# Two score slots side by side in three PSUM banks, and a second bank for filling projections

## The chip, the cores and the metric

The program runs on one core of a Trainium2 chip. Its time is the device time of one execution in microseconds (us); less is better. Each profile is of one execution, and times in it count from the start of its span. Engines are called as the profile calls them: PE (TensorE matmuls), PEld (its weight loads), DVE (VectorE), ACT (ScalarE), POOL (GpSimd), SP (the queue that issues most DMAs). PSUM, where PE puts its results, has eight banks of 512 fp32 columns on each of 128 partitions.

## The reference

Two layers of a hybrid attention trunk on 512 latent and 256 context tokens, width 1024. One input projection feeds a neighbourhood attention (branch A) and a grouped-query attention (branch B); each is gated, projected, merged by sigmoid gates, and put through one output projection. The last layer keeps no context queries. What the change touches is branch B:

```python
def _attend(q, k, v):
    s = jnp.einsum('bqkgd,btkd->bkgqt', q, k).astype(jnp.float32) * (HEAD_DIM ** -0.5)
    p = jax.nn.softmax(s, axis=-1).astype(v.dtype)
    return jnp.einsum('bkgqt,btkd->bqkgd', p, v)
...
    k_all = jnp.concatenate([ckb, kb], axis=1)
    v_all = jnp.concatenate([cvb, vb], axis=1)
    b_att = _gqa_latent(qb, k_all, v_all)
...
    out_x = _merge(a_att, b_att, a_z, b_z, g_a, g_b, w_o_a, w_o_b, w_out)
    x_new = x + gate_x * out_x
```

So each of 8 query heads has 512 latent queries over 768 keys in both layers, and in layer 0 also 256 context queries over the 256 context keys.

## The kernel before

Every fp32 product is made of three matmuls of rounded high and low parts (L435 to L437, `mm3`), accumulated in one PSUM bank. A scheduler orders each engine's instructions when the program is built, by a time model of its own; at run time each engine goes through its list strictly in that order, and an instruction that waits holds up all behind it.

The stage that changes is the grouped-query attention, once per layer (L1144 to L1206). `pipeline` (L1017) goes over the heads: the scores of head h, then the values of head h-1, then a share of `fill`, a list of projections that have nothing to do with attention at that time (gate projections, then the output projection of branch A). The fill keeps PE busy while the softmax runs elsewhere.

A **score set** is 128 queries by 768 keys, made by `gq_scores` (L1152): four matmuls on PE (L890 and L891, two of 512 columns and two of 256) into a PSUM tile `pss`; DVE reads it for the row maxima (L1161); ACT reads it for the exponential (L1162), then casts the result to a high half (`h`, L841); POOL or DVE makes the low half (L842: DVE for the first and third set of a head, POOL for the second and fourth); a DMA transposes it into `ht` (L846). A head has four such sets. In layer 0 a fifth, smaller one follows (`ctx_scores`, L896): 128 by 512, its maxima on DVE at L903, two exponentials at L909. So there are 40 sets in layer 0 and 32 in layer 1.

The values of a head (`gq_values`, L1167) are four PE transposes of the sums (`divide`, L853) and twelve matmuls (L1178, L1179) into the two banks `t`; then ACT copies one half (`ho`, L828), DVE adds (L829), POOL or DVE multiplies into `zb` (L833). In layer 0 the context values (L925) use the bank `v`. After the last head, `hilo` (L667) splits `zb` (`gbh`, `gbl`), and the output projection of branch B starts.

The eight banks in this stage: one `f` and two `t` for the whole program (L101, L102), and what `open_ps` (L1145) gives: two score tiles `s` of 1024 columns, that is of two banks each, of which a set uses 768 columns, and one bank `v`. A filling projection takes its bank from `psw()` (L116). With only `f` to take, the next one starts when ACT's tanh (L625) or DVE's product (L627, L707) has emptied it; in layer 0 one single projection gets `v` instead (L1147).

## Time and profile before

| what | value |
|---|---|
| time of three runs | 1108.36 us median, 1107.52 to 1108.36 |
| profiled execution | 1111.07 us, span 1109.3 us, mean granted PE clock 0.991 |
| busy in the span | PE 1075.5 us, DVE 767.4, ACT 617.1, POOL 473.1 |
| HBM | 115.58 MB read, 17.32 MB written |
| first to last score set, layer 0 | 375.8 to 526.7 us |
| first to last score set, layer 1 | 923.7 to 1023.6 us |

The span is the time from the first to the last instruction in the profile; the profiled execution's own time is 1.8 us more. A busy PE is one with a matmul in flight: a matmul of 512 columns takes 0.39 us from start to end, but the next one starts 0.23 us after it. So what PE could do at best is counted by starts, and a wait of PE shows as a gap between starts. Views used: the busy times by stretch, the waits of one engine, the groups of instructions by line and shape, and the instructions in order of time.

### The profile page before, as it was taken

What the parts mean: (1) busy time and instruction counts of PE and PEld (TensorE: products, weight loads), DVE (VectorE), ACT (ScalarE), POOL (GpSimd) and SP (SyncE); (2) the same over time, 40 slices, a digit from 0 to 9 for tenths busy, and PEclk for the clock granted to TensorE, in tenths of its full rate; (3) what the DMA queues carried; (4) which work ended last, traced back from release to release, by engine and by line L of the source; (5) the groups of instructions that cost most, each with busy time, mean ns of one, the idle gap of its engine ahead of it and who ended that gap; (6) DMA issues with size and microseconds to landing.
All of it is one profiled execution on the core that took longest, in us unless ns stands there. A gap on an engine that the chain in (4) does not pass through costs nothing. (4 is left out here: it accounts for less than half of the span.)

```text
span 1109.3 us, 16937 instructions
## 1 busy us (share of the span) xinstructions
PE 1075.5 (97%) x5672; PEld 879.1 (79%) x5672; DVE 767.4 (69%) x1600; ACT 617.1 (56%) x1236; POOL 473.1 (43%) x397
## 2 busy tenths in 40 slices
PE   8999999999999989989999999999999999999998
PEld 5688888788888868767788878888877888777677
DVE  4667889975377487766777785366997665677473
ACT  6454279776433566765330275444899446786430
POOL 1054235555257154463621354232355472564531
PEclk9999999999999999998999999999999999999999
DMA  9455324554543379789633542453565536879642
GB/s 370 146 171 153 90 68 111 128 138 120 169 131 127 100 184 215 166 228 228 213 101 124 157 147 78 140 163 101 134 149 130 156 107 171 199 229 239 188 152 77
DMA packets 236000, 171.79 MB, mean 155 GB/s; under 512 B 160140, under 2 KB 201864, under 8 KB 234248
## 3 DMA queue, kind: packets, MB, share of 16 engines
q1 hardware_dynamic: 228576, 156.31, 51.6%
q0 software_dynamic: 2368, 7.87, 2.1%
q10 hardware_dynamic: 4968, 6.53, 1.8%
q8 instruction: 45, 0.74, 0.3%
q14 instruction: 43, 0.35, 0.1%
HBM read 115.58 MB, written 17.32 MB: 120 GB/s over the span
## 5 line engine op out<-in xcount | busy, mean ns | idle before, releaser
L842 POOL TENSOR_TENSOR h<-p,h 128x256 f16<-128x256 f32 (+2 forms) x104 | 113.6, 1101 | 160.0 <-ACT h L841 117.7
L422 POOL TENSOR_TENSOR wlo<-raw,whi 128x512 fp32r<-128x512 f32 x70 | 98.0, 1406 | 131.6 <-ACT whi L420 98.7
L435 PE MATMUL psf<-hx,whi 128*128 128x512 f32 (+1 forms) x360 | 138.2, 384 | 2.2 <-DVE zt L627 1.2
L436 PE MATMUL psf<-hx,whi 128*128 128x512 f32 (+1 forms) x360 | 136.1, 378 | 0.0
L437 PE MATMUL psf<-hx,wlo 128*128 128x512 f32 (+1 forms) x360 | 136.1, 378 | 0.0
L435 PE MATMUL psx<-whi,hx 128*128 128x512 f32 (+1 forms) x328 | 121.0, 372 | 0.0
L437 PE MATMUL psx<-whi,hx 128*128 128x512 f32 (+1 forms) x328 | 120.0, 367 | 0.0
L420 ACT CAST whi<-raw 128x512 fp32r<-128x512 f32 x136 | 83.2, 620 | 65.5 <-DMA raw<-in_w_in_dram 46.9
L436 PE MATMUL psx<-wlo,hx 128*128 128x512 f32 (+1 forms) x328 | 119.6, 366 | 0.0
L408 POOL TENSOR_TENSOR wlo<-raw,whi 128x512 fp32r<-128x512 f32 x40 | 59.8, 1499 | 117.7 <-ACT whi L405 74.6
L405 ACT CAST whi<-raw 128x512 fp32r<-128x512 f32 x88 | 54.3, 623 | 96.7 <-PE psx L437 34.2
L508 POOL TENSOR_TENSOR ss<-ss,ehalf 128x8 f32<-128x8 f32 (+2 forms) x40 | 63.6, 1593 | 77.2 <-DVE ss L505 72.2
L841 ACT CAST h<-p 128x256 f16<-128x256 f32 (+2 forms) x136 | 81.7, 616 | 5.3 <-DMA ht<-h 1.3
L422 DVE TENSOR_TENSOR wlo<-raw,whi 128x512 fp32r<-128x512 f32 x66 | 65.3, 992 | 25.9 <-ACT whi L420 24.3
L1161 DVE CUSTOM_DVE_ANT_0 p<-pss,vb 128x768 f32<-128x768 f32 x64 | 60.2, 953 | 31.0 <-PE pss L891 28.9
L1162 ACT ACTIVATE p<-pss,mx 128x768 f32<-128x768 f32 x64 | 57.6, 901 | 41.1 <-DVE mx L1161 40.4
L435 PEld LDWEIGHTS psf<-hx,whi 128*128 128x128 f32 x360 | 68.3, 190 | 14.9 <-ACT zt L625 1.9
L437 PEld LDWEIGHTS psf<-hx,wlo 128*128 128x128 f32 x360 | 68.2, 190 | 12.0
L436 PEld LDWEIGHTS psf<-hx,whi 128*128 128x128 f32 x360 | 68.3, 190 | 10.9
L437 PEld LDWEIGHTS psx<-whi,hx 128*128 128x128 f32 x328 | 61.9, 189 | 10.2
L436 PEld LDWEIGHTS psx<-wlo,hx 128*128 128x128 f32 x328 | 62.0, 189 | 9.5
L435 PEld LDWEIGHTS psx<-whi,hx 128*128 128x128 f32 x328 | 61.8, 189 | 9.1 <-issue 0.2
(338 smaller groups left out, 2984.7 us busy)
## 6 DMA issues: line engine op xcount, KB each, us to landing
raw<-in_w_in_dram SPq DMA_DIRECT2D x168, 256.0 KB, 3.0
rawb<-in_w_ada_dram SPq DMA_DIRECT2D x48, 256.0 KB, 2.8
raw<-in_w_out_dram SPq DMA_DIRECT2D x32, 256.0 KB, 2.9
tg<-gs SPq DMA_DIRECT2D x4, 1536.0 KB, 9.9
rawx<-in_w_ada_dram SPq DMA_DIRECT2D x4, 1024.0 KB, 10.3
rawy<-in_w_ada_dram SPq DMA_DIRECT2D x4, 1024.0 KB, 10.3
gs<-zt ACTq DMA_DIRECT2D x16, 256.0 KB, 2.6
raw<-in_w_o_a_dram SPq DMA_DIRECT2D x16, 256.0 KB, 3.1
```

What stands on the lines that cost most here:

```text
L405: S.copy(hi[:, :n], raw[:, :n])
L408: e.tensor_tensor(lo[:, :n], raw[:, :n], F(hi[:, :n]), ALU.subtract)
L420: S.copy(hi, raw)
L422: lo_eng(i).tensor_tensor(lo, raw, F(hi), ALU.subtract)
L435: T.matmul(ps, lhs[0], rhs[0], start=first, stop=False)
L436: T.matmul(ps, lhs[0], rhs[1], start=False, stop=False)
L437: T.matmul(ps, lhs[1], rhs[0], start=False, stop=last)
L508: G.tensor_tensor(ss, ss, ehalf[:, :n], ALU.pow)
L841: S.copy(h[:, 0], p[:, :n])
L842: eng.tensor_tensor(h[:, 1], p[:, :n], h[:, 0], ALU.subtract)
L1161: V.tensor_tensor_reduce(p, pss, lift, -1.0, 3e38, ALU.add, ALU.min, mx[:, 0:1])
L1162: S.activation(p, pss, AF.Exp, bias=mx[:, 0:1], accum_out=r[:, i:i + 1])
```

## The change

The PSUM of the stage is laid out anew. The two score tiles (two banks each, 768 of 1024 columns used) become one tile of 1536 columns, three banks, in which slot 0 is columns 0 to 767 and slot 1 is columns 768 to 1535. Banks end at columns 512 and 1024, so slot 0 has the first bank and half of the middle one, slot 1 the other half of the middle bank and the last. Matmuls are cut at the banks' ends: slot 0 as 512 and 256 columns, slot 1 as 256 and 512. The context set of layer 0 uses the first 512 columns of whichever slot's turn it is. The bank that is left becomes `x`, a second one besides `f` for filling projections, which now take turns; the single use of `v` for one of them goes. The line in `pipeline` keeps what it did, since its test by the number of banks would no longer tell the two attentions apart. No matmul, no DVE, ACT or POOL operation and no DMA of the computation is added or taken away.

```diff
             def ctx_scores(q, kh, kl, ct, late=True):
-                pss = ps_score()
+                pss = ps_slot()[0][:, 0:512] if late else ps_score()
...
-                    att["bg"] = bg if h > 3 or pm["n"] == 1 else []
+                    att["bg"] = bg if h > 3 or last is not None else []
...
-            open_ps(s=(2, 1024), v=(1, 512))
-            if first:
-                pm["v_for"] = (2,)
+            open_ps(x=1, s=(1, 1536), v=(1, 512))
+            slots = psw(1536, "s")
+            turn_of = [0]
+
+            def ps_slot():
+
+                i = turn_of[0] % 2
+                turn_of[0] += 1
+                return slots[:, 768 * i:768 * i + 768], (512, 256)[i]
...
-                    pss = ps_score(768)
+                    pss, m = ps_slot()
                     scores(pss, q[:, 128 * i:128 * i + 128], kh, kl,
-                           [(0, 512, cut(0, 512)), (512, 256, cut(512, 768))])
+                           [(0, m, cut(0, m)), (m, 768 - m, cut(m, 768))])
```

What the scheduler makes of it shows at three places. The lines below the insertion have moved by six (the maxima from L1161 to L1167, the exponential from L1162 to L1168, the values from L1178 and L1179 to L1184 and L1185).

The first place is PE in layer 1, in the middle of the stage; in brackets stand the engines whose semaphores a row waits for. Before, in the second head:

```order
L890 MATMUL pss_2042_9989<-gk_1884_9240,qs_2039_9984 128x512 [waits PE_49,Activation_49]
L891 MATMUL pss_2042_9989<-gk_1884_9240,qs_2039_9984 128x512
L890 MATMUL pss_2042_9989<-gk_1884_9240,qs_2039_9984 128x256
L891 MATMUL pss_2042_9989<-gk_1884_9240,qs_2039_9984 128x256
L890 MATMUL pss_2046_10002<-gk_1884_9240,qs_2039_9984 128x512 [waits PE_49,Activation_49]
L891 MATMUL pss_2046_10002<-gk_1884_9240,qs_2039_9984 128x512
L890 MATMUL pss_2046_10002<-gk_1884_9240,qs_2039_9984 128x256
L891 MATMUL pss_2046_10002<-gk_1884_9240,qs_2039_9984 128x256
L853 MATMUL pst_2058_10041<-ident_90,r4_2006_9851 128x128 [waits DVE_49]
L853 MATMUL pst_2058_10041<-ident_90,r4_2006_9851 128x128 x3
L435 MATMUL psf_2075_10117<-hx_1334_6680,whi_2024_9906 128x512 [waits Activation_49]
L436 MATMUL psf_2075_10117<-hx_1336_6682,whi_2024_9906 128x512
```

Of the changed kernel, the same engine and layer, from the fifth head's third set to the sixth head's first:

```order
L890 MATMUL pss_1967_9813<-gk_1846_9205,qs_2095_10408 128x512 [waits Activation_49]
L891 MATMUL pss_1967_9813<-gk_1846_9205,qs_2095_10408 128x512
L890 MATMUL pss_1967_9813<-gk_1846_9205,qs_2095_10408 128x256
L891 MATMUL pss_1967_9813<-gk_1846_9205,qs_2095_10408 128x256
L890 MATMUL pss_1967_9813<-gk_1846_9205,qs_2095_10408 128x256 [waits Activation_49]
L891 MATMUL pss_1967_9813<-gk_1846_9205,qs_2095_10408 128x256
L890 MATMUL pss_1967_9813<-gk_1846_9205,qs_2095_10408 128x512
L891 MATMUL pss_1967_9813<-gk_1846_9205,qs_2095_10408 128x512
L890 MATMUL pss_1967_9813<-gk_1846_9205,qs_2124_10525 128x512 [waits Activation_49]
L891 MATMUL pss_1967_9813<-gk_1846_9205,qs_2124_10525 128x512
L890 MATMUL pss_1967_9813<-gk_1846_9205,qs_2124_10525 128x256
L891 MATMUL pss_1967_9813<-gk_1846_9205,qs_2124_10525 128x256
```

Before, the two sets wait for two exponentials that both lie further back (each for the last set in its own tile), and 23 matmuls of a filling projection follow. After, three sets follow each other with nothing between them, and each waits for one exponential. Followed through the semaphore's counts, this is that of the set directly before it, in the other slot; of the 72 sets 70 wait so, and before each waits for the set two back. The last filling projection of this stage now stands ahead of the fourth head's first set; before, some stood behind the last head's scores.

The second place is DVE in layer 1, where the maxima (`p,mx<-pss`) stand among the low halves (`h<-p,h`). Before, in the sixth head (`tg` is the fill's product, `wlo` the low part of a weight):

```order
L1161 ISA p_2184_10586,mx_2185_10587<-pss_2183_10581,vb_1882_9238 128x768 [waits DVE_49,PE_49]
L1161 ISA mx_2185_10587 128x1
L1161 ISA p_2188_10599,mx_2189_10600<-pss_2187_10594,vb_1882_9238 128x768 [waits PE_49,Pool_49]
L1161 ISA mx_2189_10600 128x1
L854 SCALAR_TENSOR_TENSOR zb_1995_9765<-pst_2199_10633,vb_1882_9238,zb_1995_9765 64x512 [waits PE_49]
L422 TENSOR_TENSOR wlo_2238_10802<-raw_2236_10798,whi_2237_10800 128x512 [waits DMAHW5_49,Activation_49]
L707 SCALAR_TENSOR_TENSOR tg_2177_10558<-tg_2177_10558,psf_2202_10657 128x512 [waits PE_49]
```

After, in the fifth head:

```order
L1167 ISA p_2098_10417,mx_2099_10418<-pss_1967_9813,vb_1844_9203 128x768 [waits DVE_49,PE_49]
L1167 ISA mx_2099_10418 128x1
L854 SCALAR_TENSOR_TENSOR zb_1957_9730<-pst_2110_10461,vb_1844_9203,zb_1957_9730 64x512 [waits PE_49]
L842 TENSOR_TENSOR h_2100_10421<-p_2098_10417,h_2100_10421 128x768 [waits DMAHW6_49,Activation_49]
L1167 ISA p_2101_10429,mx_2102_10430<-pss_1967_9813,vb_1844_9203 128x768 [waits PE_49,Pool_49]
L1167 ISA mx_2102_10430 128x1
L829 TENSOR_TENSOR ho_2112_10481<-pst_2111_10468,ho_2112_10481 64x512 [waits Activation_49]
L1167 ISA p_2104_10441,mx_2105_10442<-pss_1967_9813,vb_1844_9203 128x768 [waits DVE_49,PE_49]
```

The maxima stood in pairs, with the low half `h` of a set behind the pair. Now the low half of a head's first set stands between its maxima and those of the second set, and the sum `ho` of the values between the second set's and the third's; the low half of the third set stands ahead of the fourth's maxima in the same way.

The third place is PE in layer 0, at the last head's context set. Before (`psf` is the fill's bank, `gah` and `gal` are branch A):

```order
L890 MATMUL pss_1166_5779<-gk_666_3421,qs_1146_5721 128x256 [waits Activation_49]
L891 MATMUL pss_1166_5779<-gk_666_3421,qs_1146_5721 128x256
L890 MATMUL pss_1166_5779<-gk_666_3421,qs_1146_5721 128x256
L891 MATMUL pss_1166_5779<-gk_666_3421,qs_1146_5721 128x256
L435 MATMUL psf_1143_5679<-gah_1060_5308,whi_1099_5491 128x512 [waits DVE_49]
L436 MATMUL psf_1143_5679<-gal_1061_5309,whi_1099_5491 128x512
```

After:

```order
L890 MATMUL pss_818_4206<-gk_666_3421,qs_1113_5690 128x256 [waits Activation_49]
L891 MATMUL pss_818_4206<-gk_666_3421,qs_1113_5690 128x256
L890 MATMUL pss_818_4206<-gk_666_3421,qs_1113_5690 128x256
L891 MATMUL pss_818_4206<-gk_666_3421,qs_1113_5690 128x256
L853 MATMUL pst_1147_5878<-ident_90,r4_1115_5694 128x128 [waits DVE_49,PE_49]
L853 MATMUL pst_1147_5878<-ident_90,r4_1115_5694 128x128 x3
```

Before, filling projections were left for the time behind the last scores. Now all of them stand ahead of the last head's scores, and behind these come only the head's own transposes and values and the output projection of branch B.

## The prediction

> **What bounds the kernel now.** I read the page first: PE is busy nearly all the span, so PE sets the time wherever its list does not wait.

> ```profile
> span 1109.3 us, 16937 instructions
> PE 1075.5 (97%)  x5672; PEld 879.1 (79%)  x5672; DVE 767.4 (69%)  x1600; ACT 617.1 (56%)  x1236; POOL 473.1 (43%)  x397
> ```

> Then the busy times of the two stretches that run from the first score set of a layer to the last (columns: length, PE, PEld, DVE, ACT, POOL, granted clock, DMA share, GB/s).

> ```profile
> 375.00:527.00 152.00, 140.72 (x780) 114.36 (x779) 107.73 (x194) 96.92 (x188) 71.07 (x48) 0.96 0.79 194
> 924.00:1024.00 100.00, 97.90 (x469) 75.00 (x468) 70.85 (x118) 73.15 (x131) 51.12 (x33) 1.00 0.87 214
> ```

> PE is idle for 11.3 us of the first and 2.1 us of the second, 13.4 us together. That is the most that more overlap in these stages can win. Third, PE's waits, first from 370 to 560 us, then from 920 to 1040 us (total, times, longest):

> ```profile
> PE pss L890 <- ACT p L1162: 3.8, 2, 2.7
> PE pst L853 <- DVE mx L905: 2.9, 1, 2.9
> PE pss L890 <- ACT p L909: 1.3, 1, 1.3
> PE psf L435 <- DVE tg L707: 1.0, 3, 0.5
> ```

> ```profile
> PE psf L435 <- ACT zt L625: 0.9, 2, 0.6
> PE psf L435 <- DVE tg L707: 0.8, 2, 0.5
> PE pss L890 <- ACT p L1162: 0.5, 1, 0.5
> ```

> The waits for the one fill bank (the rows with `psf`) come to 1.0 + 0.9 + 0.8 = 2.7 us; those for a free score tile (`pss`) to 3.8 + 1.3 + 0.5 = 5.6 us. The other fill work around it hides the rest.

> **The price of one set that may not overlap the next.** The instruction order of the changed kernel makes 70 of 72 sets wait for the exponential of the set just before. The slots share the middle bank, and the program guards it whole. So sets become a chain, PE to DVE to ACT and back to PE. Its links are in these rows of layer 1:

> ```profile
> 1012.83 0.40 PE L890 MATMUL pss<-gk,qs 128*128 128x512 f32 x1
> ...
> 1013.42 0.28 PE L891 MATMUL pss<-gk,qs 128*128 128x256 f32 x1
> ...
> 1013.53 0.39 PE L435 MATMUL psf<-gah,whi 128*128 128x512 f32 x1
> ...
> 1013.85 0.96 DVE L1161 CUSTOM_DVE_ANT_0 p<-pss,vb 128x768 f32<-128x768 f32 x1 [0.32 <-PE pss L891]
> ...
> 1014.85 0.90 ACT L1162 ACTIVATE p<-pss,mx 128x768 f32<-128x768 f32 x1 [2.58 <-DVE mx L1161]
> ```

> ```profile
> 1021.76 0.90 ACT L1162 ACTIVATE p<-pss,mx 128x768 f32<-128x768 f32 x1 [2.70 <-DVE mx L1161]
> ...
> 1022.80 0.50 PE L890 MATMUL pss<-gk,qs 128*128 128x512 f32 x1 [0.48 <-ACT p L1162]
> ```

> Scores to maxima take 1.02 us, maxima to exponential 1.00, exponential to the next set's first matmul 1.04: 3.06 us, of which PE works 0.70 (1012.83 to 1013.53). This is the shortest chain. The order of DVE lengthens it, since the low half of a head's first and third set, and the sum `ho` of the values, now stand ahead of the next maxima:

> ```profile
> 1016.61 0.90 ACT L1162 ACTIVATE p<-pss,mx 128x768 f32<-128x768 f32 x1
> 1017.40 0.19 ACT L1162 ACTIVATION_READ_ACCUMULATOR p<-pss,mx 128x1 f32 x1
> 1017.62 0.83 ACT L841 CAST h<-p 128x768 f16<-128x768 f32 x1
> 1018.48 0.58 ACT L828 COPY ho<-pst 64x512 f32<-64x512 f32 x1
> ```

> ```profile
> L842 DVE TENSOR_TENSOR h<-p,h 128x768 f16<-128x768 f32 x16 | 18.3, 1145 | 8.9 <-ACT h L841 8.9
> L829 DVE TENSOR_TENSOR ho<-pst,ho 64x512 f32<-64x512 f32 x7 | 4.8, 685 | 2.3 <-ACT ho L828 2.3
> ```

> From an exponential to the end of its cast is 1017.62 + 0.83 - 1016.61 = 1.84 us; then the low half takes 1.15 and the next exponential follows 1.00 after its maxima begin: 1.84 + 0.04 + 1.15 + 1.00 = 4.03 us. With `ho` it is 1.84 + 0.58 + 0.69 + 1.00 and 0.09 for two handovers, 4.2 us. A head of four sets is 4.03 + 4.2 + 4.03 + 3.06 = 15.3 us. The context set of layer 0 has shorter operations but two exponentials; I estimate 3.2 us, and 18.5 us for five sets.

> **Layer 1.** PE has about enough other work for the first twelve sets (3.0 to 7.5 us between one set and the next, counted from the order). Behind the last filling projection stand twenty sets, five heads. PE's work there: twenty sets at 0.70 (14.0 us); sixty value matmuls, 0.21 apart as below (12.9); twenty transposes (four in 0.36 us: 1.8); nine early matmuls of branch B's projection at 0.23 (2.1): 30.8 us. The chain needs 5 x 15.3 = 76.5 us. The last set's 3.1 us belong to the stage's end. PE idles 76.5 - 30.8 - 3.1 = **43 us**. None of this work is new: PE does the fill earlier and then has none left.

> ```profile
> 1010.32 0.60 PE L853 MATMUL pst<-ident,r 128*128 128x128 f32 x4
> 1010.68 0.48 PE L435 MATMUL psf<-gah,whi 128*128 128x512 f32 x1
> ```

> ```profile
> 1008.17 0.38 PE L1178 MATMUL pst<-ht,vb 128*128 128x512 f16 x1
> ...
> 1008.38 0.38 PE L1179 MATMUL pst<-ht,vb 128*128 128x512 f16 x1
> ```

> **Layer 0.** The same count by places where the order leaves PE less than the chain. The fourth head, five sets with 7.2 us of PE work: 18.5 - 7.2 = 11.3. The fifth head's last three: 10.3 - 4.9 = 5.4. The seventh head's first three: 12.3 - 6.8 = 5.5. Its context set and the last head's first four: 18.5 - 9.1 = 9.4. Three sets early on, 1.9. Sum **34 us**. At the stage's end there is no fill left over the way from the last exponential through low half, transposing DMA and values; before, fill stood there. I take **4 us**, an estimate: that way is about 8 us, and PE has 3 to 4 us of transposes and values on it.

> **The clock.** PE's granted clock fell to half twice in layer 0:

> ```profile
> 407.20:410.60 3.40, 1.47 (x13) 1.27 (x11) 3.40 (x1) 0.37 (x1) 3.40 (x3) 1.00 0.51 116
> 410.60:414.00 3.40, 2.47 (x8) 1.89 (x9) 3.34 (x8) 1.93 (x6) 1.19 (x2) 0.52 0.24 77
> 414.00:417.40 3.40, 3.40 (x10) 2.72 (x9) 3.34 (x8) 2.23 (x4) 1.87 (x2) 0.50 0.92 218
> 496.00:499.40 3.40, 0.80 (x3) 0.30 (x2) 3.34 (x5) 0.23 (x1) 3.23 (x3) 1.00 1.04 403
> ```

> ```profile
> 412.64 0.79 PE L890 MATMUL pss<-gk,qs 128*128 128x512 f32 x1
> 413.23 0.63 PE L891 MATMUL pss<-gk,qs 128*128 128x512 f32 x1
> 413.66 0.41 PE L890 MATMUL pss<-gk,qs 128*128 128x256 f32 x1
> 413.87 0.41 PE L891 MATMUL pss<-gk,qs 128*128 128x256 f32 x1
> ```

> A stretch of 3.4 us with PE 43% busy (1.47 of 3.40) was followed by 6.8 us at half. A set alone keeps PE busy 0.86 us of some 3.9, 22%, so I expect half clock there. At half, a set takes 1.64 us (412.64 to 414.28) for 0.86: 0.8 more on its chain; and the 2.6 us of values take 5.2, of which 0.9 fits into the slack of their chain. A head of layer 1 would lose 4 x 0.8 + 1.7 = 4.9 us, five heads 24. In layer 0 four places lose two sets' 0.8 and one 3.4 us stretch of fill at half speed (1.7): 13. All of it is 37 us, none of it 0. The values fill PE for 2.6 us in each head and may restore the clock, so I take a little over half, **20 us**.

> [...]

> **What is won.** The 5.6 us of waits for score tiles are counted anew above, and the 2.7 us for the fill bank go: **-8 us**.

> **Sum.** 34 + 43 + 4 + 20 - 8 = 93 us. Against the profiled execution (1111 us, span 1109.3) that is 1204; the median of the runs, 1108.4, is 2.7 lower: **1201 us**. DVE, ACT and POOL do the same work, and each was busy below 75% of these stages.

> **Rivals.**

> *The second fill bank pays and the sets still overlap.* This asks that the guard ends early enough not to matter: from PE work of 3.1 to 4.2 us between sets, the chain costs nothing. Against it stand 20 sets in layer 1 with 0.7 to 3.3 us. If all idle time went, 1108 - 13 = 1095; more likely 5 us, 1103. This is the other side, **4%**.

> *No change*: chain and fill bank offset within 0.2%, which is about what a measurement here can tell: 1108, **2%**.

> *The short chain at full clock.* If DVE's low halves come early enough, every set costs 3.06 us. Set by set, PE then idles 25 us in layer 0 and 29 in layer 1: 54 + 4 - 8 = 50, so 1158. [...] For it: the best rows. Against it: the order on DVE. **22%**.

> *Half clock all through and long chains.* At 4.2 us for every set PE idles 44 + 51 = 95 us; with 37 for the clock and 4 at the end, less 2.7, it is 133: 1241. [...] **14%**.

> **Forecast and range.** The sum has **58%**. The low end is the short chain with all 13.4 us of today's idle time gone: 1108.4 + 54 - 13 = 1149, taken as 1147. The high end is the last rival, 1241. Faster by over 0.2% has 0.04, within 0.2% 0.02, slower 0.94.

> [...]

> **What would show it.** Among PE's waits, `pss` L890 on ACT L1168 should rise from 4.3 us to tens, most of it in the last five heads of layer 1. Sets there should start 3.1 to 5 us apart with one exponential between. The span from first to last set should grow from 100 to some 150 to 170 us in layer 1 and from 151 to 180 to 200 in layer 0; everything from there to the next such stage should keep its length. Waits for `psf` on `zt` or `tg` should shrink. If sets start under 3 us apart, the chain is wrong; if PE's clock stays at 1.00 there, the 20 us are.

## The result, and the profile after

The changed kernel takes **1210.36 us** (median, 1208.33 to 1213.62) against 1108.36 us before: a ratio of 1.0921, with a 95% interval of 1.0896 to 1.0946. It is slower by some 102 us; 1201 was predicted, within 1147 to 1241. The profiled execution took 1209.31 us.

The page of the changed kernel: PE's instructions are as many as before, its busy share fell from 97% to 92%, and its busy time rose by 35 us for the same matmuls. Many of these ran at a lower clock: the mean granted clock fell from 0.991 to 0.953, and a score matmul of 512 columns took 0.80 us at 1080.51, where one took 0.40 at 1012.83 before.

```profile
span 1207.5 us, 16924 instructions
...
PE 1110.5 (92%) x5672; PEld 893.7 (74%) x5672; DVE 757.8 (63%) x1600; ACT 623.0 (52%) x1236; POOL 467.5 (39%) x397
```

The busy times of the changed kernel by stretch (length, PE, PEld, DVE, ACT, POOL, granted clock, DMA share, GB/s): first to last score set of layer 0, the same of layer 1, and the last twenty sets of layer 1.

```profile
376.00:576.90 200.90, 168.78 (x882) 134.47 (x881) 111.93 (x207) 106.16 (x199) 84.10 (x58) 0.90 0.64 161
964.30:1129.00 164.70, 124.81 (x509) 87.39 (x507) 75.44 (x124) 84.19 (x144) 61.98 (x42) 0.85 0.63 149
1044.00:1128.00 84.00, 47.54 (x157) 27.34 (x157) 37.03 (x65) 39.56 (x67) 26.49 (x19) 0.72 0.51 106
```

The two stretches were 152 and 100 us long, with PE idle 11.3 and 2.1 us. Now they are 201 and 165 us, with PE idle 32.1 and 39.9 us and a granted clock of 0.90 and 0.85. In the last 84 us PE does 157 matmuls; nobody else is near full either. That is what a chain looks like: no engine is busy, since each waits for the next.

PE's waits, first from 370 to 640 us, then from 920 to 1160 us:

```profile
PE pss L890 <- ACT p L1168: 17.3, 7, 3.8
PE pss L890 <- ACT p L909: 4.8, 3, 2.8
PE psf L437 <- DVE wlo L422: 3.8, 4, 2.1
PE psv L925 <- DMA ct<-h: 3.5, 1, 3.5
```

```profile
PE pss L890 <- ACT p L1168: 29.3, 14, 3.2
PE pst L1184 <- DMA ht<-h: 7.9, 5, 4.3
PE psx L435 <- ACT p L1168: 2.8, 1, 2.8
```

The wait of a score set for an exponential rose from 3.8 and 0.5 us to 17.3 and 29.3; of the latter, 28.7 us lie in the last twenty sets. The waits of the fill bank for `tg` and `zt` are no longer among the rows. One row is new: the values (L1184) wait 7.9 us for the DMA that transposes the probabilities into `ht`.

Two links of the chain late in layer 1, on the changed kernel's instructions in order of time:

```profile
1080.51 0.80 PE L890 MATMUL pss<-gk,qs 128*128 128x512 f32 x1 [3.16 <-ACT p L1168]
...
1081.75 0.41 PE L891 MATMUL pss<-gk,qs 128*128 128x256 f32 x1
...
1082.20 0.96 DVE L1167 CUSTOM_DVE_ANT_0 p<-pss,vb 128x768 f32<-128x768 f32 x1 [1.53 <-PE pss L891]
...
1083.20 0.90 ACT L1168 ACTIVATE p<-pss,mx 128x768 f32<-128x768 f32 x1 [1.88 <-DVE mx L1167]
...
1084.24 0.58 PE L890 MATMUL pss<-gk,qs 128*128 128x256 f32 x1 [1.23 <-ACT p L1168]
...
1086.04 0.96 DVE L1167 CUSTOM_DVE_ANT_0 p<-pss,vb 128x768 f32<-128x768 f32 x1
...
1086.45 0.58 PE L1184 MATMUL pst<-ht,vb 128*128 128x512 f16 x1 [0.55 <-DMA ht<-h]
...
1087.04 0.90 ACT L1168 ACTIVATE p<-pss,mx 128x768 f32<-128x768 f32 x1 [1.99 <-DVE mx L1167]
...
1089.89 0.59 PE L890 MATMUL pss<-gk,qs 128*128 128x512 f32 x1
```

From the first matmul to the maxima it takes 1.69 us (1.02 was predicted; the granted clock was 0.51 from 1078.2 to 1088.5), from the maxima to the exponential 1.00, and from the exponential to the next set 1.04: the last two as predicted to a hundredth. The second link is longer for another reason: between that set and the next stand the values of the head before, which start at 1086.45 and hold PE to 1089.9. The exponential that frees the tile began at 1087.04; by the link of 1.04 us the set could have started at 1088.08 and started 1.8 us later.

### The profile page after: what moved, and what is told of

Read it like the earlier page. It is cut to its first block, busy times and chain, and to the rows that moved or that the text cites. A ratio compares the mean times of both kernels' runs of the same rounds, so it can differ in the third digit from the quotient of the medians.

```text
span 1207.5 us, 16924 instructions
## 1 busy us (share of the span) xinstructions
PE 1110.5 (92%) x5672; PEld 893.7 (74%) x5672; DVE 757.8 (63%) x1600; ACT 623.0 (52%) x1236; POOL 467.5 (39%) x397
## 5 line engine op out<-in xcount | busy, mean ns | idle before, releaser
L842 POOL TENSOR_TENSOR h<-p,h 128x256 f16<-128x256 f32 (+2 forms) x104 | 110.5, 1070 | 223.4 <-ACT h L841 157.3
L435 PE MATMUL psx<-whi,hx 128*128 128x512 f32 (+1 forms) x328 | 121.5, 373 | 0.0
L437 PE MATMUL psf<-hx,wlo 128*128 128x512 f32 x272 | 107.9, 397 | 2.1 <-DVE wlo L422 2.1
L1168 ACT ACTIVATE p<-pss,mx 128x768 f32<-128x768 f32 x64 | 57.7, 901 | 100.8 <-DVE mx L1167 100.6
L435 PE MATMUL psf<-hx,whi 128*128 128x512 f32 x272 | 108.0, 397 | 1.2 <-DVE zt L627 1.2
L436 PE MATMUL psf<-hx,whi 128*128 128x512 f32 x272 | 107.6, 396 | 0.0
L890 PE MATMUL pss<-gk,qs 128*128 128x256 f32 (+1 forms) x144 | 57.9, 411 | 51.6 <-ACT p L1168 46.6
L1167 DVE CUSTOM_DVE_ANT_0 p<-pss,vb 128x768 f32<-128x768 f32 x64 | 61.1, 954 | 60.5 <-PE pss L891 59.9
L437 PE MATMUL psx<-hx,wlo 128*128 128x256 f32 (+1 forms) x304 | 98.9, 325 | 0.0
L436 PE MATMUL psx<-hx,whi 128*128 128x256 f32 (+1 forms) x304 | 98.8, 325 | 0.0
L435 PE MATMUL psx<-hx,whi 128*128 128x256 f32 (+1 forms) x304 | 98.8, 325 | 0.0
L841 ACT CAST h<-p 128x256 f16<-128x256 f32 (+2 forms) x136 | 82.3, 617 | 3.9 <-DVE p L800 1.0
L422 DVE TENSOR_TENSOR wlo<-raw,whi 128x512 fp32r<-128x512 f32 x66 | 59.3, 902 | 34.0 <-ACT whi L420 33.7
L890 PEld LDWEIGHTS pss<-gk,qs 128*128 128x128 f32 x144 | 31.3, 217 | 64.8 <-ACT p L1168 55.5
L437 PEld LDWEIGHTS psx<-whi,hx 128*128 128x128 f32 x328 | 61.9, 189 | 10.4
```

The costliest lines, as they stand in the source:

```text
L422: lo_eng(i).tensor_tensor(lo, raw, F(hi), ALU.subtract)
L435: T.matmul(ps, lhs[0], rhs[0], start=first, stop=False)
L436: T.matmul(ps, lhs[0], rhs[1], start=False, stop=False)
L437: T.matmul(ps, lhs[1], rhs[0], start=False, stop=last)
L841: S.copy(h[:, 0], p[:, :n])
L842: eng.tensor_tensor(h[:, 1], p[:, :n], h[:, 0], ALU.subtract)
```

## The experiments

All were run beside the kernel before. The table has the first score matmul to the last, by layer; a longer stage can hold more fill, and then less is left for after it.

| kernel | us | ratio, 95% interval | layer 0 | layer 1 |
|---|---|---|---|---|
| before | 1108 | 1 | 150.8 | 99.7 |
| changed | 1210.4 | 1.0921, 1.0896 to 1.0946 | 200.4 | 164.2 |
| e1 slots in banks of their own, one tile, one fill bank | 1199.2 | 1.0806, 1.0774 to 1.0838 | 194.7 | 161.7 |
| e2 shared slots, one fill bank | 1196.5 | 1.0785, 1.0755 to 1.0815 | 195.0 | 157.7 |
| e3 private tiles, second fill bank in layer 1 | 1113.3 | 1.0043, 1.0028 to 1.0058 | 149.6 | 106.8 |
| e11 private tiles, second fill bank in both layers | 1114.4 | 1.0046, 1.0032 to 1.0060 | 164.1 | 107.4 |
| e4 changed, useless matmuls, free | 1223.3 | 1.1033, 1.1011 to 1.1055 | 202.2 | 176.6 |
| e5 changed, useless matmuls, tied | 1201.9 | 1.0830, 1.0809 to 1.0850 | 201.7 | 154.0 |
| e6 changed, fill tied down | 1183.6 | 1.0657, 1.0635 to 1.0680 | 206.5 | 137.3 |
| e8 changed, all low halves on POOL | 1204.6 | 1.0847, 1.0822 to 1.0872 | 204.6 | 160.4 |
| e9 changed, fill tied down evenly | 1154.6 | 1.0399, 1.0383 to 1.0414 | 183.9 | 131.8 |
| e12 as e9, one fill bank | 1157.8 | 1.0460, 1.0440 to 1.0479 | 184.6 | 139.1 |
| e7 as e3, fill tied down | 1111.3 | 1.0018, 1.0003 to 1.0032 | 152.8 | 106.7 |
| e10 before, fill tied down evenly | 1117.9 | 1.0065, 1.0048 to 1.0082 | 148.3 | 105.8 |

The theory at the outset: sets form a chain since each waits for the exponential of the set just before it, and half clock makes the chain longer. The rivals: the shared bank itself is what is guarded (e1); the second fill bank does the harm, by letting the scheduler spend the filling work early (e2, e3); the clock costs nothing (e4, e5).

### e1: one tile, but no shared bank

```diff
-            open_ps(x=1, s=(1, 1536), v=(1, 512))
-            slots = psw(1536, "s")
+            open_ps(s=(1, 2048), v=(1, 512))
+            if first:
+                pm["v_for"] = (2,)
+            slots = psw(2048, "s")
...
-                return slots[:, 768 * i:768 * i + 768], (512, 256)[i]
+                return slots[:, 1024 * i:1024 * i + 768], 512
```

> The slots get banks of their own (columns 0 and 1024 of one tile of four banks), and the second fill bank goes, so that only one thing is left of the change: both slots are parts of one tile. If the guard goes by the tile, each set still waits for the exponential just before it, and the time is that of the changed kernel, 1210 us, plus 2 to 6 us for the missing second fill bank: 1210 to 1216, with 72 sets in a chain. If the guard goes by the bank (the prediction's wording: the shared middle bank is what is guarded), sets overlap as before and the time is that of the kernel before, 1108 us, within 3.

It took 1199.2 us, so the guard goes by the tile. PE's waits of this kernel from 920 to 1160 us:

```profile
PE pss L890 <- ACT p L1170: 20.1, 10, 2.8
```

In layer 1 no set of e1 starts sooner than 1.04 us after the exponential of the set just before it (1.03 in the changed kernel); in the kernel before, 16 of 31 start ahead of that exponential. The banks of e1 are laid out as in the kernel before, each slot in two of its own; all that differs is that the two slots are cut from one tile. That alone costs 91 us (1199.2 - 1108.3). The prediction's reason, "the slots share the middle bank, and the program guards it whole", had the wrong object: the whole tile is guarded, shared bank or not. The time is below the 1210 that I had expected, which e2 explains.

### e2, e3, e11: the second fill bank by itself

e2 is the changed kernel with one fill bank, e3 the kernel before with a second fill bank in layer 1 (in place of the bank `v`, unused there), e11 the same in both layers. In layer 0 of e11 the context values must then use the banks `t`, so that only e3 changes nothing but the fill bank.

```diff
 e2
-            open_ps(x=1, s=(1, 1536), v=(1, 512))
+            open_ps(s=(1, 1536), v=(1, 512))
+            if first:
+                pm["v_for"] = (2,)
 e3, from the kernel before
-                    att["bg"] = bg if h > 3 or pm["n"] == 1 else []
+                    att["bg"] = bg if h > 3 or last is not None else []
...
-            open_ps(s=(2, 1024), v=(1, 512))
             if first:
+                open_ps(s=(2, 1024), v=(1, 512))
                 pm["v_for"] = (2,)
+            else:
+                open_ps(x=1, s=(2, 1024))
 e11, from the kernel before
-                ps = psw(512 if late else 256, "v" if late or not att["spare"] or pm["n"] > 1 else "s")
+                ps = psw(512 if late else 256, "t" if late else "v" if not att["spare"] or pm["n"] > 1 else "s")
...
-                    att["bg"] = bg if h > 3 or pm["n"] == 1 else []
+                    att["bg"] = bg if h > 3 or last is not None else []
...
-            open_ps(s=(2, 1024), v=(1, 512))
-            if first:
-                pm["v_for"] = (2,)
+            open_ps(x=1, s=(2, 1024))
```

> The shared slots of the change, but with one fill bank as before. Chain theory: the loss is all in the slots, and the second fill bank wins at most the 2.7 us of waits that the profile before showed: 1210 to 1214 us. Rival: the second fill bank lets PE run ahead through the filling work, so that none is left for the last five heads; without it the fill would last longer and the time would fall well below, to 1150 to 1190 us.

> The kernel before with its two private score tiles; in layer 1 alone the bank that stood unused there serves as a second fill bank. Chain theory: no chain, and the second bank wins the waits for the fill bank in that stage, 0.9 + 0.8 = 1.7 us at most: 1106 to 1109 us, between 2 us less and no change. Rival (the second fill bank spends the fill too early): 1120 us or more, with waits for a score tile in the last heads.

> Private score tiles, and a second fill bank in both layers in place of the bank v (the context values of layer 0 use the banks t instead). It is the second fill bank without the chain, to be set beside the changed kernel with one and with two fill banks (1196 and 1210 us). If the second bank does harm only where sets wait for each other, 1104 to 1110 us; if it does harm by itself because the scheduler brings the fill forward, 1113 to 1122 us.

In e2 and e3 neither expectation had the second bank right; e11 came out at its second, harm by the bank itself. With the slots in one tile, one fill bank takes 1196.5 us and two take 1210.4; with private tiles, one takes 1108 and two 1113.3 or 1114.4. The second bank **costs** 14 us with the chain (ratios 1.0785 and 1.0921) and about 5 without it (ratios 1.0043 and 1.0046). The rows that it was to remove do exist with one bank; PE's waits of e2 from 370 to 640 us:

```profile
PE pss L890 <- ACT p L1170: 9.3, 9, 2.2
PE psf L435 <- DVE tg L707: 5.3, 5, 2.0
PE psf L435 <- ACT zt L625: 4.8, 4, 3.3
```

Those 10.1 us for the fill bank are gone in the changed kernel, and yet it is slower. What moved is the order. These are the fill matmuls behind each of the 32 sets of layer 1, up to the last set, counted from the order of PE's instructions (one of 256 columns counts half; behind the long rows of zeros of e2 and the changed kernel, the 1, 5 and 3 are early matmuls of branch B's own projection):

```
before   0 24  0 24  0 23  0  1  0 24  0 24  0 14  0 10  0 24  0 12  0 12  0 12 12  0  9  3 10  0  2
e2      24 24 24 24 22  2 22 24 12 14 12 12 12 12 12 12  1  0  0  0  0  0  0  0  5  0  0  3  0  0  0
changed 28 28 29 28 21 22 10 20 24 16 20 12  1  0  0  0  0  0  0  0  0  0  0  0  5  0  0  3  0  0  0
e9      12 12 12 12  6  6  6  6 12 12 12 12  6  6  6  6 12 12 12 12  9  9  9  9  9  9  9  9  6  6  6
```

Each set waits for the one before, and the scheduler fills the gap with more than it needs: 28 matmuls are 6.4 us (28 x 0.23) in a gap of some 2.4 us (3.06 - 0.70). With a second bank it finds still more that can start, and the fill ends four sets earlier. That is the order with the chain; why the second bank costs 5 us without it stays open.

### e4, e5: the clock

Both add 120 useless matmuls, whose result nobody reads, to the last five heads of layer 1. In e4 the scheduler was free to place them; in e5 they are tied to the last score matmul of their set.

```diff
 e4 and e5
+            spare = None if first else psw(512, "v")
...
+                att["head"] = h
...
 e4
+                    if not first and att["head"] > 2:
+                        for _ in range(6):
+                            T.matmul(spare, kh[:, 0:128], kh[:, 0:512], start=True, stop=True)
                     turned(p, 768, ht[:, i], G if i in SPLIT_POOL else V)
 e5, behind scores(...) of the set
+                    if not first and att["head"] > 2:
+                        behind(ON_PE, lambda: [T.matmul(spare, kh[:, 0:128], kh[:, 0:512], start=True, stop=True)
+                                               for _ in range(6)])
```

> The changed kernel; behind every set of the last five heads of layer 1 PE also runs six useless matmuls of 128x512 into a bank that nobody reads (1.4 us at full clock, of 3 to 4 us from one set to the next), 120 in all. If half clock is a term of the loss, as the prediction has it (24 us in layer 1 if it held there throughout), the granted clock stays at 1.00 in that stage, sets come 3.1 to 4.1 us apart, and the time falls by 12 to 22 us, to 1188 to 1198. If the chain alone sets the distance of the sets and the clock costs nothing, the time stays at 1210 us or rises by up to 5 us.

e4 took 1223.3 us and says nothing of the clock: by the order of PE's instructions the scheduler moved the useless matmuls, which wait for nothing, behind the fifth to the fourteenth set, where fill stood already. The last sets stayed bare, at a granted clock of 0.72 from 1077 to 1144 us. It is one more case of work placed early: 28 us of it (120 x 0.23) made the kernel 13 us longer.

> The changed kernel with the same 120 useless matmuls as in the run before (six of 128x512 after each set of heads four to eight of layer 1, into a bank that nobody reads), but now tied to the last score matmul of their set, so that the scheduler cannot move them to the front of the stage. PE is then busy 2.1 of some 3.1 to 4.1 us. If half clock is a term of the loss: granted clock 1.00 from 1045 to 1130 us, the set-to-set distance inside a head 3.1 to 4.1 us with the fourth link shorter, and 10 to 20 us less than the changed kernel, 1190 to 1200 us. If only the chain counts: 1208 to 1215 us, with the useless matmuls in the gaps.

e5 took 1201.9 us, 8.5 less than the changed kernel though PE did 28 us more. The last twenty sets of e5:

```profile
1043.00:1120.00 77.00, 61.41 (x282) 42.10 (x283) 39.15 (x68) 42.51 (x73) 27.96 (x19) 1.00 0.53 122
```

The clock is 1.00 where the changed kernel had 0.72. Its heads start 15.8, 15.5, 15.8 and 16.9 us apart; in the changed kernel it is 20.5, 17.8, 16.9 and 18.1. So half clock is a term of the loss and costs some 9 us in layer 1, net of what the useless matmuls themselves may hold up, and the chain by itself takes close to the predicted 15.3 us per head. Not all of its links are those of the prediction, though. A head in e5:

```profile
1077.87 0.39 PE L890 MATMUL pss<-gk,qs 128*128 128x256 f32 x1 [0.26 <-ACT p L1172]
...
1078.71 0.96 DVE L842 TENSOR_TENSOR h<-p,h 128x768 f16<-128x768 f32 x1 [0.32 <-ACT h L841]
...
1079.59 0.95 DVE L1171 CUSTOM_DVE_ANT_0 p<-pss,vb 128x768 f32<-128x768 f32 x1
...
1080.76 0.38 PE L1188 MATMUL pst<-ht,vb 128*128 128x512 f16 x1 [0.56 <-DMA ht<-h]
...
1083.15 0.58 PE L890 MATMUL pss<-gk,qs 128*128 128x512 f32 x1
```

The low half on DVE (L842) does stand in the maxima's way, 0.7 us here (1079.59 instead of 1077.87 + 1.02). But the longest link, 5.3 us from 1077.87 to 1083.15, is that in which PE has the twelve value matmuls ahead of the next set. From exponential to exponential this head takes 3.76, 5.24, 3.76 and 3.04 us, 15.8 in all, where 4.03, 4.2, 4.03 and 3.06 were predicted.

### e8: the low halves off DVE

```diff
-SPLIT_POOL = (1, 3)
+SPLIT_POOL = (0, 1, 2, 3)
```

> The changed kernel with the low halves of all four sets of a head on POOL, so that none stands on DVE between two maxima. Long-chain theory of the prediction: two sets in each head get shorter by 4.03 - 3.06 = 0.97 us, 10 us over the last five heads and some 6 in layer 0: 1192 to 1202 us. If DVE's low half is not what ends the wait for the maxima (at half clock the scores alone take 1.65 us), nothing is won: 1207 to 1213 us.

1204.6 us: less than the changed kernel by 0.7% (ratios 1.0847 and 1.0921), between the two expectations. A set of e8 at half clock (its first matmul of 512 columns takes 0.79 us), without any low half on DVE:

```profile
1075.86 0.79 PE L890 MATMUL pss<-gk,qs 128*128 128x512 f32 x1 [2.22 <-ACT p L1168]
...
1077.09 0.42 PE L891 MATMUL pss<-gk,qs 128*128 128x256 f32 x1
...
1077.65 0.96 DVE L1167 CUSTOM_DVE_ANT_0 p<-pss,vb 128x768 f32<-128x768 f32 x1 [0.98 <-PE pss L891]
```

The maxima come 1.79 us after the first matmul, as late as with the low half ahead of them (1.80 in the changed kernel, 1084.24 to 1086.04 above): this set's scores end only at 1077.51 (1077.09 + 0.42), 1.65 us after their start. The two delays lie side by side, so that their prices do not add up. In a set of e8 at full clock (its matmuls of 512 columns take 0.39 us) the maxima come after 1.14 us (1106.68 to 1107.82), against 1.72 in e5 with the low half ahead of them; there the move pays.

### e6, e9, e12, e10, e7: the same chain, the fill held back

In these the fill matmuls of a head are cut in as many parts as the head has marked sets, and no part may be placed ahead of its set. e6 gives each head its share by the number of projections, as the changed kernel does, and marks only the four large sets of a head; e9 shares by matmuls and marks the context sets of layer 0 too. e7 is tied as e6 is; e10 and e12 are tied as e9 is.

```diff
+    def spread_out(fn, marks):
+
+        n = len(nc.cur_bb.bb.instructions)
+        fn()
+        pe = [i for i in nc.cur_bb.bb.instructions[n:] if i.engine == ON_PE]
+        before = None
+        for k, i in enumerate(pe):
+            for last in {marks[k * len(marks) // len(pe)], before} - {None}:
+                tc.add_manual_dep(i, last, mybir.DependencyInfo(
+                    mybir.DependencyClass.NoSync, mybir.DependencyReason.DATA), reason="program order")
+            before = i.name
...
+                    att["marks"] = att["marks"] + latest(ON_PE, 1)
...
-                    run(fill, len(fill) - (n - n * min(h + 1, spread) // spread))
+                    upto = (0, 4, 8, 12, 15, 19, 25, 33, 40) if first else (0, 3, 5, 8, 9, 14, 18, 22, 24)
+                    k = len(fill) - (n - n * min(h + 1, spread) // spread) if last is None else upto[h + 1] - upto[h]
+                    if last is None:
+                        run(fill, k)
+                    else:
+                        spread_out(lambda: run(fill, k), att["marks"])
...
+                    att["marks"] = ([] if i == 0 else att["marks"]) + latest(ON_PE, 1)
```

(The second part, in `ctx_scores`, is not in e6, and e6 has the third part without `upto`.)

> The changed kernel, slots, guard and both fill banks as they are; only the filling work is tied down: the matmuls that a head is given are cut in four (five in layer 0) and each part may not start before the head's next set has been issued. By the program's order 3 to 12 fill matmuls then follow every set of layer 1, where the changed kernel has 20 to 29 behind each of the first sets and none behind the last twenty. If the loss comes from fill that is spent too early, the chain is hidden behind 0.7 + 0.7 + 3 to 12 x 0.23 us of work per set: idle time of some 15 us in layer 1 and 15 to 25 in layer 0, full clock, 1130 to 1155 us. If each set costs its chain wherever the fill stands, the time stays above 1190 us.

e6 took 1183.6 us, between the two. Layer 1 fell from 164 to 137 us; layer 0 stayed at 206, with a granted clock of 0.89. In layer 0 the shares were still 24, 12, 24, 12, 0 in the first head and 6 to 12 in the last, with none behind any context set, since e6 does not mark these (the "five in layer 0" of the expectation is not what the edit does). In layer 1 the shares were 12 for sixteen sets and then 3 to 9. The expected 15 us of idle time in layer 1 and 15 to 25 in layer 0 had left that out. In PE's waits from 370 to 640 us, the longest row of e6 is that of the context sets' exponentials:

```profile
PE pss L902 <- ACT p L921: 17.0, 6, 5.2
```

> The changed kernel with the fill tied down as in the run with 1184 us, but shared out by matmuls and not by the number of projections, so that every set of layer 1 has 6 to 12 fill matmuls behind it up to the end and every set of layer 0 has 6 to 15. Chain theory: a head of layer 1 takes what the run with useless matmuls showed at full clock, 15.8 us, or its PE work if that is more: 126 to 132 us for the stage, from 164; layer 0 is set by PE's work of some 4.1 us per set, 165 to 180 us from 200: 1140 to 1165 us in all, with the granted clock at 1.00. If something else than fill spent early holds PE up in layer 0 (there the run with 1184 us stayed at 206 us), layer 0 stays above 195 us and the time above 1170 us.

e9 took **1154.6 us**, as the chain theory had it, and the row of the context sets fell to 5.2 us. Its two stages:

```profile
370.00:554.70 184.70, 162.68 (x881) 129.73 (x881) 116.19 (x205) 102.98 (x198) 75.90 (x55) 0.96 0.70 174
940.00:1072.40 132.40, 113.65 (x523) 82.14 (x524) 74.93 (x124) 81.55 (x142) 58.13 (x39) 1.00 0.72 184
```

Slots, guard, banks and matmuls are those of the changed kernel; only the order is another, and 56 of the 102 us are gone. Layer 1 takes 132 us, against 8 x 15.8 = 126 for eight heads of the bare chain. Layer 0 was a few us above its forecast, at a granted clock of 0.96 and not 1.00; whether the even shares or the marks of the context sets brought it down from 206 us was not tried separately. PE's waits of e9 from 930 to 1130 us (its lines have moved by 12 and more):

```profile
PE pss L902 <- ACT p L1187: 16.5, 14, 3.2
PE pst L1203 <- DMA ht<-h: 1.9, 2, 1.0
```

> The run with 1155 us (shared slots, fill tied down and shared out evenly), but with one fill bank in place of two. Since the fill cannot be brought forward here, it shows what the second bank is worth by itself. If a second bank only lets projections follow each other without a wait, as the prediction had it, its lack costs the waits for the fill bank: 1157 to 1165 us. If the second bank is worth nothing or does harm beyond bringing the fill forward, 1148 to 1155 us.

Here the second fill bank could show what it is worth, since no fill can be brought forward. e12 took 1157.8 us at a ratio of 1.0460 (1.0440 to 1.0479), e9 has 1.0399 (1.0383 to 1.0414): the second bank wins 3 us by the medians, some 7 by the ratios. PE's waits of e12 from 360 to 640 us:

```profile
PE psf L435 <- DVE tg L719: 8.7, 9, 4.5
...
PE pss L902 <- ACT p L1189: 3.7, 8, 1.4
PE psf L435 <- ACT zt L637: 3.5, 6, 0.7
```

The 12 us for the fill bank are not among the rows of e9. But its layer 0 is hardly shorter (183.9 us against 184.6), since the sets there wait longer for their exponentials instead (14.6 us against 3.7, over the same 360 to 640 us). The difference shows in layer 1, 131.8 us against 139.1, where 4.4 us of e12's waits are for the fill bank. So a second bank does remove these waits, as the prediction reasoned, but only part of them turns into time, less than the order that it was paid with.

> The kernel before, private score tiles and one fill bank, with the fill tied down in the same way. It shows what tying down costs or wins by itself. Its sets overlap, so the place of the fill should matter little: 1104 to 1110 us, at best some 4 of the 13.4 us of idle time won. If tying the fill down costs by itself (projections cut into pieces hold the one fill bank longer), 1115 us or more.

> Two private score tiles as in the kernel before, the unused bank of layer 1 as a second fill bank, and the fill tied down as in the run above. The second fill bank alone cost 5 us (1113). If that came from fill spent early, it goes, and a little of the 13.4 us of idle time before goes too: 1102 to 1108 us. If the second bank costs by itself, 1111 to 1116 us.

Neither beat the kernel before. e10 took 1117.9 us, the upper expectation: with private tiles the sets need no fill between them, and the waits for the one fill bank grew, as cut projections hold it longer (PE's waits of e10 from 360 to 540 us):

```profile
PE psf L435 <- DVE tg L719: 5.8, 6, 2.9
```

It was 1.0 us before. e7 took 1111.3 us, at a ratio of 1.0018 (1.0003 to 1.0032), at the low edge of its upper expectation. That is less than e3 (1.0028 to 1.0058) by so little that it does not settle whether the 5 us of the second bank went with the order. No version was found that is faster than the kernel before.

## Why the prediction was right, and where it was not

**The price of one set that may not overlap.** Right in its size and in most of its links: 1.00 and 1.04 us were met to a hundredth, and a head at full clock took 15.5 to 16.9 us (e5) for 15.3. In the head shown, the two links with the low half on DVE took 3.76 us for 4.03, and the short one 3.04 for 3.06. The link with `ho` took 5.24 for 4.2: the prediction was wrong in what makes it long, not `ho` on DVE but the values on PE, which wait for a transposing DMA. It was wrong, too, in the object of the guard (e1): the tile is guarded, not the shared bank. Two separately guarded slots in one bank were not tried.

**Layer 0 and layer 1.** From the first scores of layer 0 to the first attention of the next layer the kernel took 437.8 us instead of 399.9, 37.9 longer; the terms for that, 34 + 4, with 13 of 37 parts of the clock's 20 and less 6.1 of the waits won, make 39. From there to the last matmul it took 388.9 instead of 329.4, 59.5 longer, for 43 + 13 - 2.2 = 54. The prediction said "PE does the fill earlier and then has none left". That sentence carries more than its place suggests: e9 shows that 56 us hang on the order, the clock's dips among them. Some 45 remain (1154.6 - 1109.2): the chain that this order does not hide, and what tying the fill down costs by itself (7 to 9 us in e10). How they divide was not tried.

**The parts of the sum.** The span grew by 98 us. PE's idle time in it grew from 33.8 to 97.0 us, by 63, and PE's busy time for the same matmuls by 35. The sum had 34 + 43 + 4 - 8 = 73 of idle time and 20 for the clock. So the total, 93, is nearer than its two parts, which is partly luck.

**The clock.** 20 us were taken for both layers, of which layer 1 has 13; e5 measured some 9 there. The direction was right, the size half again too high, since the chain has other delays beside which the slower scores lie (e8); for the same reason the 35 us of longer busy time are not what the clock costs. Layer 0's part was not tried by itself. The granted clock was 0.72 over the last 84 us of layer 1's sets. It fell twelve times after the kernel's start. At one of these falls PE has no matmul between 470.7 and 474.5 us; at the other eleven PE was busy 0.97 to 1.54 us of the 3.41 us before.

**What is won.** This step failed: "the 2.7 us for the fill bank go". The waits did go, but the second bank cost 14 us (e2) where it was put down as a gain, because the scheduler placed the fill still earlier for it. The total came out right all the same, since the 34 and 43 us had been counted in the changed kernel's order, in which this harm was already contained. With the fill held in place the bank does win 3 to 7 us (e9 against e12).

**The stage end.** Its 4 us were an estimate. Between the last scores of layer 0 and the first of layer 1's stage PE is idle for 8.9 us instead of 5.5, 3.4 more, which is near it. But the sign that this part "should keep its length" failed: it took 387.9 us instead of 397.2. It has 99 matmuls fewer, for the fill that now stands ahead of the last scores is missing behind them. For the same reason the length of a stage alone overstates the loss.

**The other signs.** The waits of `pss` rose to tens, most in the last five heads, and the stages took 200.4 and 164.2 us, at the upper end of one forecast and within the other. Of the nineteen distances between the last twenty sets, fourteen lie between 3.1 and 5 us; the five longer ones, up to 9.9, are those with the values in them.

**The rivals.** That the sets still overlap, or that the effects cancel out, is excluded by the waits and by the time. The short chain at full clock (1158) had its price for a set right for some sets only; that e9 ends near that number has another reason, a changed order. Half clock all through (1241) was half true: the clock came back between dips (0.99 from 1054.30 to 1061.20 us).

## What to carry to other kernels

Two buffers cut from one tile may be one buffer to the program's guard: check whether each user waits for the use just before or for that two back. Where an engine is full because filling work hides a latency, count how much filling work each gap needs and hold the rest back; a scheduler that fills every gap as far as it can leaves the last gaps bare. And a freed buffer given to the filling work changes the order, whose price can exceed the waits that it removes.

## What the runs showed of the hardware

The granted clock fell late in layer 1 behind stretches in which PE had work. The changed kernel by stretches there:

```profile
1040.70:1044.10 3.40, 1.65 (x10) 1.07 (x8) 2.75 (x6) 2.92 (x6) 1.34 (x2) 1.00 0.90 205
1044.10:1054.30 10.20, 5.38 (x12) 2.23 (x13) 4.01 (x7) 3.90 (x7) 3.18 (x2) 0.51 1.17 247
1054.30:1061.20 6.90, 3.01 (x14) 1.73 (x12) 2.93 (x5) 3.02 (x5) 1.26 (x1) 0.99 0.07 16
1061.20:1071.40 10.20, 6.70 (x19) 3.75 (x20) 4.97 (x10) 5.47 (x9) 1.75 (x2) 0.50 0.51 116
1071.40:1078.20 6.80, 3.17 (x15) 1.79 (x13) 2.26 (x4) 3.33 (x6) 2.80 (x2) 0.99 0.26 58
```
